# Small fp32 products on quarters of TensorE's array, and weights split before a layer's last products

## The chip, the core and the metric

The kernel is one program on one NeuronCore of a Trainium2 chip. The metric is device time in microseconds; before the change the median of three runs is 2081.71 (2081.35 to 2082.46). The engines are TensorE (PE in the profile, with its weight loads shown apart as PEld), VectorE (DVE), ScalarE (ACT), GpSimd (POOL) and SyncE (SP), which issues nearly all transfers.

## The reference, cut to what matters

Two blocks of two layers each work on a sequence of 512 tokens of width 1024; layer 0 also carries 256 tokens of context. Block one conditions both layers on a vector (`mod`). Block two adds a state space mixer, a gated linear recurrence and two feed-forward parts.

```python
# layer 0: window attention and a gated convolution, for the latent and the context tokens
mod = silu(c) @ w_ada[l] + b_ada[l]            # shift, scale, gate
q, k, v, g_a, xb, b_g, c_g, g_b = split((x * (1 + scale) + shift) @ w_in)
p = softmax([sink, q @ kc.T, q @ k_window.T]); o_a = p @ [vc, v_window]
x = layer_norm(ALPHA * x + gate * (concat(o_a * silu(g_a), o_b * silu(g_b)) @ w_out))
# layer 1: gated recurrence over chunks, S_t = diag(f_t) S_(t-1) + k_t v_t^T, both directions
# layer 2 (even): dilated attention, and a state space model over 32 groups
bu = einsum('gpc,bsgc->bsgp', b_bar, u); h = scan(a_bar, bu); y = einsum('gcp,bsgp->bsgc', c_mat, h).real
x = x + rms_norm(concat(att, ssm) @ w_out)
x = x + rms_norm((silu(xn @ w_gate) * (xn @ w_up)) @ w_down)
# layer 3 (odd): convolution, gates, scan  h_t = a_t h_(t-1) + b_t ; then a second feed-forward part
```

## The kernel before

Activations stand transposed, features on the 128 partitions and tokens along the free dimension, in tiles of 128 features. A large product is exact to about fp32 by a split: a tile `t` is held as `hi`, rounded to fp32r, and `lo = t - hi`, and `product` (three `matmul` calls for each of 8 tiles) adds hi x hi, hi x lo and lo x hi in one PSUM bank. The stationary operand is a 128x128 piece of a weight block, the moving one 512 or 256 columns of an activation tile. `weights` loads a block (512 KB) into a raw buffer `wp_r` (three of them), ScalarE copies it to `wp_h`, and VectorE or GpSimd subtracts to make `wp_l` (four buffers each).

Small products are left in fp32: the attention's probabilities times values (`po`, in `attend` of layer 0 and of the even layer), the conditioning's selection sums (`self.sel`, in `ada`), the state space kernels (`Xm` times `Cm`, in `matrices`), and the state space chunk states (`G` times `U`, in `s5_quarter`). Each is one `matmul` with a 128x128 stationary operand and 64, 2, 16 and 64 moving columns. The products of `ada` (L431) and the scores of layer 1's scans (L963) already use quarters: `tile_position=(0, 32 * k)` places a stationary operand of 32 columns in one of four column groups of the array, and its output on 32 partitions.

A layer ends in `out_products`. The first weight blocks run over all 512 columns; the last three (`keep`) run over columns 0 to 255 and then 256 to 511, so that `done` can normalise the first half while the second is multiplied. `done` needs the sum over all features of the squares (accumulated by VectorE in `po_a` or `n_a`), which TensorE forms with a matrix of ones (bank `z`). Its loop over eight tiles writes the new residual `res_x` and calls `pre`, which makes the next layer's `act_h` and `act_l`. The next layer begins in `firsts` with three blocks over the first half and then over the second, tile by tile, as the tiles become ready. The row statistic (`rms`: ones times `res_acc`, bank `z` or `g`) comes after them, since a row's factor can be applied behind a product.

The order of instructions on each engine is made by a scheduler from the program's order, priorities and its own estimates; every engine then runs its list in order, and waits on semaphores. SBUF tiles are allotted in pools, one behind the other, in steps of 32 bytes; pools of `side="right"` from the upper end.

Of the kernel before, what the change touches and what calls it, by code (L numbers as in the profile page):

```python
# [189 lines left out]
class Prog:  # L190
    def __init__(self, es, tc, I, off):
        self.tc, self.nc, self.I, self.off, self.es = tc, tc.nc, I, off, es
        nc = self.nc
        self.const = es.enter_context(tc.tile_pool(name="const", bufs=1))
        self.wp = Alloc(es, tc, "wp", {"r": (3, 1024), "h": (4, 1024), "l": (4, 1024)})
        self.dram = es.enter_context(tc.tile_pool(name="dram", bufs=1, space=bass.MemoryType.DRAM))
        self.banks = es.enter_context(
            tc.tile_pool(name="banks", bufs=1, reuse_waits="tile", space=bass.MemoryType.PSUM)
        )
        self.clock = count()  # L200
        self.used = {f"b{i}": next(self.clock) for i in range(8)}
# [103 lines left out]
    def firsts(self, ps, blocks, xs, tags=("mm",) * 3):  # L305


        ws = [self.weights(b, eng=self.nc.gpsimd) for b in blocks]
# [7 lines left out]
        return list(zip(out, ws))  # L316

# [27 lines left out]
    def out_products(self, ps, block, xs, parts, use, done, keep=3, n=1024, late=(), begun=None, spare=(None, 0)):  # L345
# [21 lines left out]
        ws = [self.weights(block(8 - keep + j), n, pool=pool if j < own else None) for j in range(keep)]  # L367
        last = iter(())
# [28 lines left out]
    def conditioning(self, es):  # L397
# [13 lines left out]
        self.sel = cond.tile([128, 2], F32, name="sel")  # L411
# [9 lines left out]
    def ada(self, l, i, p, pool=None):  # L421
# [21 lines left out]
        def finish(t=t):  # L443
# [3 lines left out]
            for a in range(2):  # L447
                self.matmul(o[:, a], t[:, a * 128:(a + 1) * 128], self.sel)
# [5 lines left out]
    def layer0(self, stop=False):  # L454

        nc, tc = self.nc, self.tc
        with ExitStack() as es:
# [78 lines left out]
            self.out_products(ps, lambda m: self.I["wo_ab"][m], xs2, PARTS, use, done, spare=(Alloc(es, tc, "w0", {"h": (1, 1024), "l": (1, 1024)}), 1))  # L536

    def layer0_mix(self, es, e0, late, xs, Y, first, s5):
# [65 lines left out]
        def attend(qT, j, n, ctx, y, sg):  # L604
# [130 lines left out]
        for j in range(4):  # L735
            ys[j] = Y("y") if j else late("y")
            cv = conv(j)
            for i in range(6):
# [80 lines left out]
    def layer1(self):  # L819
        nc, tc = self.nc, self.tc  # L820
        with ExitStack() as es:
# [24 lines left out]
            self.out_products(ps, lambda m: self.I["wo_c"][m], xs2, PARTS[:2], use, done, spare=(Alloc(es, tc, "w5", {"h": (1, 1024), "l": (1, 1024)}), 1))  # L846
# [252 lines left out]
    def prenorm(self, es, ps, name, l):  # L1099
# [8 lines left out]
        def pre(k, s, x=None, scale=g, bias=None):  # L1108
            hi, lo = self.xs[k]
# [123 lines left out]
    def s5_prepare(self, prep):  # L1233
# [111 lines left out]
        def matrices(half):  # L1345
# [3 lines left out]
            for e in range(8):  # L1349
# [27 lines left out]
                for g in range(4):  # L1377
                    self.matmul(p[:, g * 16:(g + 1) * 16], Xm[:, g * 128:(g + 1) * 128], Cm[:, g * 16:(g + 1) * 16])
# [18 lines left out]
    def s5_quarter(self, q, S, ps, ut, y):  # L1397
# [67 lines left out]
    def even(self):  # L1465
        tc = self.tc
        with ExitStack() as es:
# [6 lines left out]
            self.out_products(ps, lambda m: self.I["wo_ev"][m], xs2, PARTS[:2], use, done, late=(4, 5), begun=begun, spare=(Alloc(es, tc, "w6", {"h": (2, 1024), "l": (2, 1024)}), 2))  # L1474
            stats()

    def even_mix(self, es, e1, Y):
# [47 lines left out]
        def attend(kz, vn, qT, y, n):  # L1525
# [27 lines left out]
            for h, T in enumerate(Ts):  # L1553
                b = slice(64 * h, 64 * h + 64)
                for i in range(n + 1):
                    s = slice(i * 128, (i + 1) * 128)
                    self.matmul(po[:, b], T[:, s], vn[:, i * 128 + 64 * h:i * 128 + 64 * h + 64], i == 0, i == n)
# [130 lines left out]
    def odd(self):  # L1688
        tc = self.tc
        with ExitStack() as es:  # L1690
# [6 lines left out]
            self.out_products(ps, lambda m: self.I["wo_od"][m], xs2, PARTS[:2], use, done, late=(2, 4), spare=(Alloc(es, tc, "w7", {"h": (3, 1024), "l": (3, 1024)}), 3))  # L1697
            stats()

    def odd_mix(self, es, B):  # L1700
        nc, tc, xs, r = self.nc, self.tc, self.xs, self.rr
        A = Alloc(es, tc, "o7", {
            "sp2": (1, 8), "hb": (1, 16), "h": (4, L), "l": (4, L), "xb": (2, L + 3), "xc": (2, 1024),
# [5 lines left out]
        sp2, hb = A("sp2"), A("hb")  # L1709
# [79 lines left out]
        first = dict(enumerate(self.firsts(ps, self.od[:3], xs)))  # L1789
        self.rms(ps("g"))  # L1790
# [30 lines left out]
    def ffn(self, l, last=None):  # L1821

        nc, tc, xs, r = self.nc, self.tc, self.xs, self.rr
        with ExitStack() as es:
# [16 lines left out]
            for a, b in ((0, 6), (6, 14), (14, 22)):  # L1841
# [30 lines left out]
                else:  # L1872
# [5 lines left out]
                    self.out_products(ps, block, hs, PARTS[:2], use, done, n=n, keep=4 if last else 3, spare=(H, 2))  # L1878
# [65 lines left out]
```

## Time and profile before

| | |
|---|---|
| runs | 2081.35, 2082.46, 2081.71 us; median 2081.71 |
| profiled execution | 2084.1 us; its span 2082.1, 33162 instructions |
| busy: PE, PEld | 2008.2 us (96%), 1699.2 us (82%) |
| busy: DVE, ACT, POOL | 1307.2 us (63%), 955.9 us (46%), 386.9 us (19%) |
| granted TensorE clock, mean | 0.986 |
| DMA | 246.75 MB, 119 GB/s on average |

A TensorE instruction's duration is modelled and holds its latency, so busy times of neighbouring instructions overlap; the pace is read from start to start. An fp32 product is two instructions in the trace and one in the listed order. The chain that ended last names TensorE for 33% of the span, of which 32% is the line of `matmul` (L319).

### The profile page before, as it was taken

How to read it: one execution, taken by the hardware profiler on the slowest of the kernel's cores; microseconds unless marked ns; L12 is line 12 of the kernel's file. 1: busy time of each engine (PE TensorE's matmuls, PEld its weight loads, DVE VectorE, ACT ScalarE, POOL GpSimd, SP SyncE). 2: the span in 40 equal slices, each digit the busy share in tenths (PEclk: the TensorE clock that was granted, in tenths of full speed). 3: DMA queues.
4: the chain of work that ended last, by engine and by line, in shares of the span. 5: the costliest groups of instructions: out<-in, count | busy, mean ns of one | idle time of the engine just before them, and what ended most of it. 6: DMA issues, size and time to landing. Idle time of an engine off the chain costs nothing. (4 is left out here: it accounts for less than half of the span.)

```text
span 2082.1 us, 33162 instructions
## 1 busy us (share of the span) xinstructions
PE 2008.2 (96%) x13160; PEld 1699.2 (82%) x13160; DVE 1307.2 (63%) x2318; ACT 955.9 (46%) x1730; POOL 386.9 (19%) x383
## 2 busy tenths in 40 slices
PE   6999999999999999989999999999989999999997
PEld 4888888888888888788878878888888888888886
DVE  6775556787656665786655855544568775354455
ACT  2564333446555555554655644322346654322231
POOL 1111111335223221142102310101020131010011
PEclk9999999999999999999989999999999999999998
DMA  8344432322111111325423589333435323323331
GB/s 305 117 158 147 148 125 92 110 74 87 52 52 54 60 52 52 112 73 162 121 67 106 181 320 324 126 96 95 138 113 182 117 86 96 106 92 101 101 102 41
DMA packets 91818, 246.75 MB, mean 119 GB/s; under 512 B 20624, under 2 KB 29712, under 8 KB 91664
## 3 DMA queue, kind: packets, MB, share of 16 engines
q1 hardware_dynamic: 91664, 244.65, 35.7%
q8 instruction: 103, 1.69, 0.3%
q14 instruction: 51, 0.42, 0.1%
HBM read 209.48 MB, written 35.13 MB: 117 GB/s over the span
## 5 line engine op out<-in xcount | busy, mean ns | idle before, releaser
L245 ACT ACTIVATE wp_h<-wp_r 128x1024 fp32r<-128x1024 f32 (+2 forms) x243 | 250.9, 1037 | 416.5 <-PE mm L319 263.2
L251 DVE TENSOR_TENSOR wp_l<-wp_r,wp_h 128x1024 fp32r<-128x1024 f32 (+1 forms) x228 | 315.2, 1385 | 123.3 <-ACT wp_h L245 119.2
L319 PE MATMUL mm<-act_l,wp_h 128*128 128x512 f32 (+1 forms) x1008 | 378.9, 376 | 4.7 <-POOL act_l L251 4.7
L319 PE MATMUL mm<-act_h,wp_h 128*128 128x512 f32 (+1 forms) x1008 | 377.4, 375 | 2.5 <-ACT act_h L245 2.5
L319 PE MATMUL mm<-act_h,wp_l 128*128 128x512 f32 (+1 forms) x1008 | 377.3, 374 | 0.0
L319 PE MATMUL mm<-a_h,wp_h 128*128 128x512 f32 (+1 forms) x920 | 334.8, 365 | 5.1 <-ACT wp_h L245 3.1
L319 PE MATMUL mm<-a_h,wp_l 128*128 128x512 f32 (+1 forms) x920 | 330.1, 359 | 1.2 <-POOL wp_l L251 1.2
L319 PE MATMUL mm<-a_l,wp_h 128*128 128x512 f32 (+1 forms) x920 | 329.1, 358 | 0.6 <-DVE a_l L251 0.6
L319 PEld LDWEIGHTS mm<-act_l,wp_h 128*128 128x128 f32 x1008 | 192.3, 191 | 38.7 <-POOL act_l L251 5.8
L319 PEld LDWEIGHTS mm<-act_h,wp_h 128*128 128x128 f32 x1008 | 191.8, 191 | 35.7 <-ACT act_h L245 2.9
L319 PEld LDWEIGHTS mm<-act_h,wp_l 128*128 128x128 f32 x1008 | 192.1, 191 | 32.8 <-issue 1.0
L319 PEld LDWEIGHTS mm<-a_h,wp_h 128*128 128x128 f32 x920 | 174.1, 189 | 31.6 <-issue 3.6
L319 PEld LDWEIGHTS mm<-a_l,wp_h 128*128 128x128 f32 x920 | 174.3, 189 | 26.2 <-issue 2.3
L319 PEld LDWEIGHTS mm<-a_h,wp_l 128*128 128x128 f32 x920 | 174.0, 189 | 25.2 <-POOL wp_l L251 1.4
L251 POOL TENSOR_TENSOR g_g<-g_g,g_u 128x512 f32<-128x512 f32 x44 | 63.1, 1435 | 550.4 <-DVE g_u L251 493.7
L319 PE MATMUL mm<-h_h,wp_h 128*128 128x512 f32 (+1 forms) x344 | 129.0, 375 | 2.1 <-ACT h_h L245 2.1
L319 PE MATMUL mm<-h_l,wp_h 128*128 128x512 f32 (+1 forms) x344 | 129.2, 376 | 0.6 <-DVE h_l L251 0.5
L319 PE MATMUL mm<-h_h,wp_l 128*128 128x512 f32 (+1 forms) x344 | 128.8, 374 | 0.0
L251 DVE TENSOR_TENSOR g_u<-mm,res_rr 128x512 f32<-128x512 f32 x44 | 30.3, 689 | 110.5 <-PE mm L319 110.5
L248 ACT ACT_TABLE_LOAD x60 | 77.0, 1283 | 1.8 <-PEq L1932 0.7
L319 PEld LDWEIGHTS mm<-h_h,wp_h 128*128 128x128 f32 x344 | 64.8, 188 | 14.6 <-ACT h_h L245 3.0
L251 POOL TENSOR_TENSOR act_l<-pn_h,act_h 128x256 fp32r<-128x256 f32 x64 | 57.5, 919 | 102.6 <-ACT act_h L245 102.2
(505 smaller groups left out, 3819.2 us busy)
## 6 DMA issues: line engine op xcount, KB each, us to landing
wp_r<-w_gu SPq DMA_DIRECT2D x88, 512.0 KB, 3.6
wp_r<-w_c SPq DMA_DIRECT2D x40, 512.0 KB, 3.3
wp_r<-wada SPq DMA_DIRECT2D x32, 512.0 KB, 3.7
wp_r<-w_d SPq DMA_DIRECT2D x32, 512.0 KB, 3.5
wp_r<-w_ab SPq DMA_DIRECT2D x26, 512.0 KB, 4.6
od_d<-z_h SPq DMA_DIRECT2D x20, 512.0 KB, 3.6
od_d<-z_l SPq DMA_DIRECT2D x20, 512.0 KB, 4.0
wp_h<-od_d SPq DMA_DIRECT2D x20, 512.0 KB, 3.7
```

Source lines behind the costliest of these rows:

```text
L245: self.nc.scalar.activation(out=out, in_=in_, func=ACT.Copy, scale=scale)
L248: self.nc.scalar.activation(out=out, in_=in_, func=func, **kw)
L251: (eng or self.nc.vector).tensor_tensor(out=out, in0=a, in1=b, op=op)
L319: self.nc.tensor.matmul(out=out, lhsT=a, rhs=b, start=start, stop=stop)
```

## The change

Five things are done. `quarters` replaces `matmul` in the five small products above: four products with 32 stationary columns each, in the four column groups, over the same moving operand. `out_products` takes `after`, weight blocks of the next layer; behind the last blocks it loads and splits as many as buffers allow (`4 - keep + own`: two where one pair of spare buffers exists, else three) and `firsts` takes these over. `pre` writes the high part directly where there is no bias, with the low part as one VectorE step, and no longer uses GpSimd. In layer 0's attention a `yield` stands ahead of the value products, and the conditioning work `more_ada` is called between the two. The odd layer forms its fourth product before its statistics. Beside these, `rope2` gets a pool of its own at the upper end, and `dummy`, `sel` and `sp2` are padded to 16 elements.

```diff
-        self.rope2 = self.const.tile([128, 4], F32, name="rope2")
+        self.edge = es.enter_context(tc.tile_pool(name="edge", bufs=1, side="right"))
+        self.rope2 = self.edge.tile([128, 4], F32, name="rope2")
-        self.dummy = self.const.tile([128, 1], F32, name="dummy")
+        self.ahead = []
+        self.dummy = self.const.tile([128, 16], F32, name="dummy")[:, 0:1]
...
-        ws = [self.weights(b, eng=self.nc.gpsimd) for b in blocks]
+        ws = self.ahead + [self.weights(b, eng=self.nc.gpsimd) for b in blocks[len(self.ahead):]]
+        self.ahead = []
...
+    def quarters(self, out, a, b, start=True, stop=True):
+        for k in range(4):
+            s = slice(32 * k, 32 * k + 32)
+            self.nc.tensor.matmul(out=out[s], lhsT=a[:, s], rhs=b, start=start, stop=stop, tile_position=(0, 32 * k))
...
         ws = [self.weights(block(8 - keep + j), n, pool=pool if j < own else None) for j in range(keep)]
+        self.ahead = [self.weights(b) for b in after[:4 - keep + own]]
...
-        self.sel = cond.tile([128, 2], F32, name="sel")
+        sel = cond.tile([128, 16], F32, name="sel")
+        self.sel = sel[:, 0:2]
...
-                self.matmul(o[:, a], t[:, a * 128:(a + 1) * 128], self.sel)
+                self.quarters(o[:, a], t[:, a * 128:(a + 1) * 128], self.sel)
...
+            yield
             po = aux[:, 256:512]
...
-                    self.matmul(po[:, b], r, vn[:, tiles[i], b], i == 0, i == nk - 1)
+                    self.quarters(po[:, b], r, vn[:, tiles[i], b], i == 0, i == nk - 1)
...
-                more_ada()
                 if j:
                     next(mats, None)
+                next(at)
+                more_ada()
...
-            h = N("h")
             if bias is None:
-                self.act(h, x, ACT.Copy, scale=scale[:, k:k + 1])
+                self.act(hi, x, ACT.Copy, scale=scale[:, k:k + 1])
+                self.stt(lo, x, scale[:, k:k + 1], hi.bitcast(F32), ALU.mult, ALU.subtract)
             else:
+                h = N("h")
                 self.act(h, x, ACT.Identity, scale=scale[:, k:k + 1], bias=bias[:, k:k + 1])
-            self.copy(hi[:, s], h)
-            self.sub(lo[:, s], h, hi[:, s].bitcast(F32), nc.gpsimd)
+                self.copy(hi, h)
+                self.sub(lo, h, hi.bitcast(F32))
...
-                    self.matmul(p[:, g * 16:(g + 1) * 16], Xm[:, g * 128:(g + 1) * 128], Cm[:, g * 16:(g + 1) * 16])
+                    self.quarters(p[:, g * 16:(g + 1) * 16], Xm[:, g * 128:(g + 1) * 128], Cm[:, g * 16:(g + 1) * 16])
...
-            self.matmul(p[:, s], G[:, g], U[:, s])
+            self.quarters(p[:, s], G[:, g], U[:, s])
...
         first = dict(enumerate(self.firsts(ps, self.od[:3], xs)))
+        first[3] = proj(3), None
         self.rms(ps("g"))
```

The calls of `out_products` get `after` with the next layer's first three blocks, in the order in which `firsts` takes them; the even layer's value product changes as layer 0's does, and `sp2` is padded like `sel`.

On TensorE, in layer 0's attention before: `mc<-sel` are the selection sums, `mc<-wp_r,sc` the conditioning products, `pt` the transposes of the probabilities, `S` the scores, `x<-m_vn,m_T` the value products, `mm` a projection.

```order
L319 MATMUL mc<-sel,adat_t 128x2 x2
L657 MATMUL pt<-idn,m_P 128x128 x3
L431 MATMUL mc<-wp_r,sc 32x256 x8
L657 MATMUL pt<-idn,m_P 128x128
L319 MATMUL S<-m_kz,m_qs 128x256 x7
L657 MATMUL pt<-idn,m_P 128x128 x4
L319 MATMUL x<-m_vn,m_T 128x64 x4
L319 MATMUL S<-m_kz,m_qs 128x256
L319 MATMUL mm<-a_h,wp_h 128x512
L319 MATMUL mm<-a_l,wp_h 128x512
L319 MATMUL x<-m_vn,m_T 128x64 x4
```

The same place now:

```order
L670 MATMUL pt<-idn,m_P 128x128 x4
L326 MATMUL mc<-sel,adat_t 32x2 x8
L329 MATMUL S<-m_kz,m_qs 128x256 x3
L444 MATMUL mc<-wp_r,sc 32x256
L670 MATMUL pt<-idn,m_P 128x128 x4
L444 MATMUL mc<-wp_r,sc 32x256 x7
L326 MATMUL x<-m_vn,m_T 32x64 x32
L329 MATMUL S<-m_kz,m_qs 128x256 x5
L329 MATMUL mm<-a_h,wp_h 128x512
```

The value products of both heads stand together behind the conditioning products, in quarters as these are, and scores follow; before they stood in two groups with a score and a projection between them.

On VectorE, at the end of the first feed-forward part before, where the second half's normalisation begins: `po_t` and `po_r` are the reciprocal root, `g_ff` the mixed rows, `res_x` the residual.

```order
L267 SCALAR_TENSOR_TENSOR res_x<-g_ff,vecs,res_x 128x256
L267 SCALAR_TENSOR_TENSOR po_t<-z,po_r 128x256
L267 SCALAR_TENSOR_TENSOR po_t<-po_t,po_r 128x256
L267 SCALAR_TENSOR_TENSOR po_r<-po_t,po_r 128x256
L251 TENSOR_TENSOR g_ff<-g_ff,po_r 128x256 x2
L267 SCALAR_TENSOR_TENSOR res_x<-g_ff,vecs,res_x 128x256 x2
L251 TENSOR_TENSOR g_ff<-g_ff,po_r 128x256 x2
L267 SCALAR_TENSOR_TENSOR res_x<-g_ff,vecs,res_x 128x256 x2
L251 TENSOR_TENSOR g_ff<-g_ff,po_r 128x256 x2
L267 SCALAR_TENSOR_TENSOR res_x<-g_ff,vecs,res_x 128x256 x2
```

The same place now:

```order
L270 SCALAR_TENSOR_TENSOR res_x<-g_ff,vecs,res_x 128x256 x2
L270 SCALAR_TENSOR_TENSOR po_t<-z,po_r 128x256
L270 SCALAR_TENSOR_TENSOR act_l<-res_x,vecs,act_h 128x256 x2
L270 SCALAR_TENSOR_TENSOR po_t<-po_t,po_r 128x256
L270 SCALAR_TENSOR_TENSOR po_r<-po_t,po_r 128x256
L254 TENSOR_TENSOR g_ff<-g_ff,po_r 128x256 x2
L270 SCALAR_TENSOR_TENSOR res_x<-g_ff,vecs,res_x 128x256 x2
L254 TENSOR_TENSOR g_ff<-g_ff,po_r 128x256
L270 SCALAR_TENSOR_TENSOR act_l<-res_x,vecs,act_h 128x256 x2
L270 SCALAR_TENSOR_TENSOR res_x<-g_ff,vecs,res_x 128x256
L254 TENSOR_TENSOR g_ff<-g_ff,po_r 128x256 x2
L270 SCALAR_TENSOR_TENSOR act_l<-res_x,vecs,act_h 128x256
```

The steps that write `act_l`, which stood on GpSimd, now stand on VectorE between the residual's.

## Rows read from the trace of the kernel before

**Rows 1.** Windows: stretch and length, busy us of PE, PEld, DVE, ACT, POOL, clock, DMA.
```profile
85.00:392.00 307.00, 306.35 (x2199) 263.02 (x2198) 192.69 (x535) 143.57 (x364) 38.91 (x50) 1.00 0.40 130
500.00:862.00 362.00, 357.03 (x3925) 301.92 (x3924) 232.73 (x421) 200.29 (x366) 84.82 (x85) 1.00 0.18 57
905.00:930.00 25.00, 19.08 (x132) 17.69 (x131) 19.14 (x37) 14.99 (x34) 17.91 (x18) 0.93 0.30 93
1066.00:1087.00 21.00, 19.89 (x87) 18.13 (x87) 10.77 (x31) 7.70 (x26) 1.39 (x2) 0.51 0.08 26
1532.00:1562.00 30.00, 23.11 (x148) 20.40 (x147) 23.67 (x42) 15.99 (x36) 10.40 (x14) 0.89 0.36 136
```

**Rows 2.** Groups by line and form: shapes, count, busy us, mean ns, idle before.
```profile
L319 PE MATMUL x<-m_vn,m_T 128*128 128x64 f32 x352 | 44.8, 268 | 0.0
...
L319 PE MATMUL o<-e_vn,e_T 128*128 128x64 f32 x160 | 25.2, 302 | 0.6 <-ACT y_y L245 0.6
...
L319 PE MATMUL mc<-sel,adat_t 128*128 128x2 f32 x64 | 8.5, 238 | 0.0
...
L963 PE MATMUL a<-m_qp,m_km 128*32 128x64 f32 x256 | 5.4, 224 | 0.1
...
L319 PEld LDWEIGHTS x<-m_vn,m_T 128*128 128x128 f32 x352 | 44.4, 191 | 2.1 <-DVE m_st L626 0.4 <-DVE m_T L669 0.3
```

**Rows 3.** Timeline, weight loads of layer 0's value products: start, us for all.
```profile
305.94 0.98 PEld L319 LDWEIGHTS x<-m_vn,m_T 128*128 128x128 f32 x8
```

**Rows 4.** Timeline, TensorE in layer 1's scores: whole array, quarters, whole array.
```profile
617.44 0.28 PE L319 MATMUL mm<-a_h,wp_l 128*128 128x256 f32 x1
617.65 1.03 PE L963 MATMUL a<-m_qm,m_km 128*32 128x32 f32 x96
618.52 0.68 PE L963 MATMUL a<-m_qp,m_km 128*32 128x64 f32 x32
...
619.47 0.40 PE L319 MATMUL mm<-a_l,wp_h 128*128 128x512 f32 x1
```

**Rows 5.** Timeline, first and 24th of 512-column steps over a and over act.
```profile
872.45 0.40 PE L319 MATMUL mm<-a_h,wp_l 128*128 128x512 f32 x1
...
877.84 0.39 PE L319 MATMUL mm<-a_l,wp_h 128*128 128x512 f32 x1
...
1934.60 0.39 PE L319 MATMUL mm<-act_h,wp_h 128*128 128x512 f32 x1
...
1939.81 0.39 PE L319 MATMUL mm<-act_h,wp_l 128*128 128x512 f32 x1
```

**Rows 6.** Timeline, first and 24th of 256-column steps over a and over act.
```profile
312.79 0.28 PE L319 MATMUL mc<-a_h,wp_h 128*128 128x256 f32 x1
...
315.47 0.28 PE L319 MATMUL mc<-a_h,wp_l 128*128 128x256 f32 x1
...
1708.20 0.28 PE L319 MATMUL mm<-act_h,wp_l 128*128 128x256 f32 x1
...
1710.95 0.28 PE L319 MATMUL mm<-act_l,wp_h 128*128 128x256 f32 x1
```

**Rows 7.** Waits of TensorE over the whole span: us, times, longest us.
```profile
PE z L319 <- DVE po_a L251: 8.6, 5, 2.6
...
PE mm L319 <- POOL act_l L251: 4.7, 5, 1.2
...
PE g L319 <- DVE res_acc L251: 3.4, 1, 3.4
...
PE o L319 <- DVE res_x L267: 2.9, 1, 2.9
```

**Rows 8.** Timeline, VectorE and GpSimd at the end of the first feed-forward part.
```profile
1540.44 0.76 DVE L251 TENSOR_TENSOR g_ff<-g_ff,po_r 128x256 f32<-128x256 f32 x2
...
1541.52 5.26 POOL L251 TENSOR_TENSOR act_l<-pn_h,act_h 128x256 fp32r<-128x256 f32 x5 [3.32 <-ACT act_h L245]
...
1544.33 1.85 DVE L251 TENSOR_TENSOR g_ff<-g_ff,po_r 128x256 f32<-128x256 f32 x2
```

More of the change, by code (lines that the diff above doesn't have):

```diff
@@ L343, in scores, with out_products @@
             self.matmul(out, q[h], k[:, cols], i == 0, i == 1)
-    def out_products(self, ps, block, xs, parts, use, done, keep=3, n=1024, late=(), begun=None, spare=(None, 0)):
+    def out_products(self, ps, block, xs, parts, use, done, keep=3, n=1024, late=(), begun=None, spare=(None, 0), after=()):
         wide = [X] + [s for s in parts if s.start >= L]
@@ L535, in layer0 @@
             use, done = self.deepnorm(N, ps, res, mod, emit)
-            self.out_products(ps, lambda m: self.I["wo_ab"][m], xs2, PARTS, use, done, spare=(Alloc(es, tc, "w0", {"h": (1, 1024), "l": (1, 1024)}), 1))
+            self.out_products(ps, lambda m: self.I["wo_ab"][m], xs2, PARTS, use, done, spare=(Alloc(es, tc, "w0", {"h": (1, 1024), "l": (1, 1024)}), 1), after=[self.I["w_c"][m] for m in range(3)])
     def layer0_mix(self, es, e0, late, xs, Y, first, s5):
@@ L845, in layer1 @@
             use, done = self.deepnorm(N, ps, self.x, self.mods[1], emit)
-            self.out_products(ps, lambda m: self.I["wo_c"][m], xs2, PARTS[:2], use, done, spare=(Alloc(es, tc, "w5", {"h": (1, 1024), "l": (1, 1024)}), 1))
+            self.out_products(ps, lambda m: self.I["wo_c"][m], xs2, PARTS[:2], use, done, spare=(Alloc(es, tc, "w5", {"h": (1, 1024), "l": (1, 1024)}), 1), after=[self.I["w_ev"][m] for m in (4, 8, 0)])
             for k in range(KT):
@@ L1108, in pre @@
         def pre(k, s, x=None, scale=g, bias=None):
-            hi, lo = self.xs[k]
-            h = N("h")
+            hi, lo = (t[:, s] for t in self.xs[k])
             x = self.x[k][:, s] if x is None else x
             if bias is None:
-                self.act(h, x, ACT.Copy, scale=scale[:, k:k + 1])
+                self.act(hi, x, ACT.Copy, scale=scale[:, k:k + 1])
+                self.stt(lo, x, scale[:, k:k + 1], hi.bitcast(F32), ALU.mult, ALU.subtract)
             else:
+                h = N("h")
                 self.act(h, x, ACT.Identity, scale=scale[:, k:k + 1], bias=bias[:, k:k + 1])
-            self.copy(hi[:, s], h)
-            self.sub(lo[:, s], h, hi[:, s].bitcast(F32), nc.gpsimd)
+                self.copy(hi, h)
+                self.sub(lo, h, hi.bitcast(F32))
         def stats():
@@ L1473, in even @@
             use, done = self.postnorm(es, ps, "norm_mix_post", 0, pre)
-            self.out_products(ps, lambda m: self.I["wo_ev"][m], xs2, PARTS[:2], use, done, late=(4, 5), begun=begun, spare=(Alloc(es, tc, "w6", {"h": (2, 1024), "l": (2, 1024)}), 2))
+            self.out_products(ps, lambda m: self.I["wo_ev"][m], xs2, PARTS[:2], use, done, late=(4, 5), begun=begun, spare=(Alloc(es, tc, "w6", {"h": (2, 1024), "l": (2, 1024)}), 2), after=[self.I["w_gu0"][m] for m in range(3)])
             stats()
@@ L1556, in attend @@
                     s = slice(i * 128, (i + 1) * 128)
-                    self.matmul(po[:, b], T[:, s], vn[:, i * 128 + 64 * h:i * 128 + 64 * h + 64], i == 0, i == n)
+                    self.quarters(po[:, b], T[:, s], vn[:, i * 128 + 64 * h:i * 128 + 64 * h + 64], i == 0, i == n)
             o = E("o")
@@ L1696, in odd @@
             use, done = self.postnorm(es, ps, "norm_mix_post", 1, pre)
-            self.out_products(ps, lambda m: self.I["wo_od"][m], xs2, PARTS[:2], use, done, late=(2, 4), spare=(Alloc(es, tc, "w7", {"h": (3, 1024), "l": (3, 1024)}), 3))
+            self.out_products(ps, lambda m: self.I["wo_od"][m], xs2, PARTS[:2], use, done, late=(2, 4), spare=(Alloc(es, tc, "w7", {"h": (3, 1024), "l": (3, 1024)}), 3), after=[self.I["w_gu1"][m] for m in range(3)])
             stats()
@@ L1702, in odd_mix @@
         A = Alloc(es, tc, "o7", {
-            "sp2": (1, 8), "hb": (1, 16), "h": (4, L), "l": (4, L), "xb": (2, L + 3), "xc": (2, 1024),
+            "sp2": (1, 16), "hb": (1, 16), "h": (4, L), "l": (4, L), "xb": (2, L + 3), "xc": (2, 1024),
             "tr": (2, 1024), "ti": (2, 1024), "a": (2, L), "mu": (2, L), "u": (2, 1024), "z": (2, 1024),
@@ L1708, in odd_mix @@
         sp = self.sp
-        sp2, hb = A("sp2"), A("hb")
+        sp2, hb = A("sp2")[:, 0:8], A("hb")
         self.ts(sp2, sp, 2.0, ALU.mult)
@@ L1877, in ffn @@
                     use, done = self.postnorm(es, ps, "norm_ffn_post", l, pre, ff, last)
-                    self.out_products(ps, block, hs, PARTS[:2], use, done, n=n, keep=4 if last else 3, spare=(H, 2))
+                    self.out_products(ps, block, hs, PARTS[:2], use, done, n=n, keep=4 if last else 3, spare=(H, 2), after=() if last else self.od[:3])
                     if stats:
```

## The prediction

> **What bounds the kernel now.** I read the busy times by stretch first [rows 1]. In layer 0's attention (85 to 392 us) TensorE is busy for 306 of 307 us, in layer 1's scans for 357 of 362; VectorE has 193 and 233, ScalarE less. So there the time is the number of TensorE's instructions times their pace, and what makes them cheaper shortens the run directly. The passage from the first feed-forward to the odd layer (1532 to 1562) is different: TensorE is busy for 23 of 30 us, at a granted clock of 0.89. The list of TensorE's waits says for what [rows 7]: 8.6 us in five waits for the running sum that the last normalisation needs (po_a), 4.7 for the low parts act_l that GpSimd makes, 3.4 for res_acc before the row statistics, 2.9 for a bank that VectorE frees late. These 19.6 us lie where layers meet.
>
> Second, the small fp32 products [rows 2]. The trace has two instructions for each product, so the 352 of x<-m_vn,m_T are 176 products of attention values in layer 0, and the 160 of o<-e_vn,e_T 80 in the even layer. Three groups of 64 instructions, 32 products each, are the conditioning sums mc<-sel in layer 0's attention, the state space kernels mc<-s_C there and the chunk states s<-s_U,s_G in the even layer (the first stands for the three). Together 352 products, 704 instructions. They have 2 to 64 moving columns, and yet cost alike: eight weight loads take 0.98 us [rows 3], one lasts 0.191 [rows 2], so the pace is (0.98 - 0.19) / 7 = 0.113 us each. They pay for loading 128 columns, not for what streams past.
>
> Third, the pace of the long products [rows 5]. Twenty-four steps of 512 columns over the tiles a (layers 0 and 1) take 877.84 - 872.45 = 5.39 us between first and last, over the tiles act 1939.81 - 1934.60 = 5.21: 234 and 227 ns, with the same weights' tiles. In the built program the tiles a, b (layers 0 and 1, the even and odd outputs) and o7 begin 32 bytes past a multiple of 64; act and h begin on a multiple. 234 / 227 is 33 / 32, as if a row of 2048 bytes were fetched in pieces of 64 and one that begins in the middle needed one more. That reading is mine, from these two paces.
>
> **The change part by part.** *Quarters.* Each of the 352 products becomes four on 32 columns each, so 8 instructions. Layer 1's scores already work so: 96 of 32 moving columns go from 617.65 to 618.52, 9.1 ns each, and 32 of 64 columns last 0.68 us, of which one alone lasts 0.224: (0.68 - 0.22) / 31 = 14.8 ns [rows 2, 4]. Before: 704 x 0.113 = 79.6 us. After: 288 products of 64 columns x 8 x 14.8 ns = 34.1 us, 64 narrow ones x 8 x 9.1 = 4.7; gross gain 40.8 us.
>
> The same rows price the switch between whole array and quarters. From the last whole product (617.44) to the second one behind the block (619.47) are 2.03 us; the block's own are 0.87 + 0.47, two ordinary products 0.12 + 0.23 [rows 5, 6]; 0.34 us are left for going in and out. Read off the program's order, TensorE enters quarters 71 times instead of 20 in layer 0's attention and 27 times instead of never in the even layer: 78 x 0.34 = 26.5 us. Net 14.3 us. The narrow ones have no row of their own; with 9.1 to 14.8 ns they make up to 2.9 us less. With the switch at 0.24 to 0.44 the net is 4 to 22 us. The conditioning sums before the attention I count at nothing: that stretch waits for transfers of weights.
>
> On the price of a quarter the Trainium skill (TensorE: Matmul & The Clock Gate, section "Wait — 56ns, not 53.3ns?") speaks against the change: start to start never falls below about 25 ns, however small the product. By that, an estimate, 2816 quarters would take 70 us, and the net be a loss of 17. The trace does not agree where four column groups run side by side: 9.1 and 14.8 ns [rows 4].
>
> *Addresses.* The padding of dummy, sel and sp2 and the move of rope2 look idle, but they shift what is allotted behind them: in the built program a, b and o7 now begin on multiples of 64. 2088 instructions of 512 columns stream from them. At the difference of [rows 5], 0.18 us in 23 steps, that is 7.8 ns each, 16 us. The 256-column products go the other way: 23 steps over a take 315.47 - 312.79 = 2.68 us, over act 1710.95 - 1708.20 = 2.75 [rows 6], 3.0 ns more, and 2112 of them stream from the moved tiles: 6.3 us lost, if the address is the reason there too (their pace is near that of weight loads, so it may not be). I take the lower, 16.3 - 6.3 = 10, of which I count 9; ends 0 and 16.
>
> *Between layers.* Three things happen. (a) Three weight blocks (two where only one spare pair of buffers exists) are split on ScalarE and VectorE ahead of the last products, no longer on GpSimd behind them. (b) The low parts act_l move from GpSimd to VectorE, and ScalarE writes the high part in one step instead of two. (c) The odd layer does its fourth product before its statistics.
>
> For (a) and (b) VectorE gets 16 instructions per passage at the 0.38 us of an undisturbed one (two in 0.76), 6.1 us. It loses a disturbance: while GpSimd makes act_l (5.26 us for five), two of VectorE's last 1.85 [rows 8]. GpSimd is busy for 10.4 us of that passage, which slows some 11 of VectorE's by 0.55: 6 us. So VectorE ends about when it did. But TensorE has more in front of the wait: in the order z<-po_a stands behind 36, 30 and 30 first products instead of 29, 19 and 19, 29 x 0.12 = 3.5 us of the 8.6. Of the 4.7 us for act_l I take half, 2.4: the chain is one hop shorter, but VectorE makes them at 3 x 0.4 us per tile against 1.08 us that TensorE needs for nine products. Of the 2.9 us for the bank, held up by a weight split on GpSimd, 1.5, since the third block there is still GpSimd's. For (c): 24 products x 0.227 = 5.4 us now cover the 3.4 us, but then the reciprocal root and its three VectorE steps stand uncovered, because the four banks hold products that wait for it; net 2. The clock: 0.89 over 30 us means 30 x 0.11 x 2 = 6.6 us at half clock, and 0.93 over 25 us (layer 1 to the even layer, [rows 1]; the passages behind the even and the odd mixer read alike) 3.5 each, 17 us in all, and idle stretches stand before them. If half of it stays away, that is 8.5 us and gives back at most half, 4.3; some of it is waiting anyway, so 3. Sum 12.4; ends -4 (VectorE late in each passage) and 26 (all waits and most of the half clock).
>
> The added waits: SyncE now issues the ahead transfers in front of the next layer's, and each must find one of three raw buffers free; ScalarE's split waits for that transfer with squares and act_h queued behind it. The cover is the wide products just before, 24 x 0.227 = 5.4 us each, with VectorE half idle. Without that cover each block would cost its split, some 1 us. The new yield in the attention moves the value products behind the conditioning work; it lets the transposes' copies finish and costs nothing.
>
> **Sum.** The profiled execution took 2084.1 us, 2.0 more than its span and 2.4 more than the median of 2081.7. 2084.1 - 14.3 - 9 - 12.4 = 2048.4; less 2.4, 2046 as a median.
>
> **The rivals.** *VectorE becomes the bound at the passages* (15%). For: it is busy for 23.7 of 30 us there and gets all low parts. Against: GpSimd's disturbance goes. The 12.4 become -4: 2062.
> *The pace does not follow the address* (9%). For: only two kinds of tiles are compared, and 256 columns say the opposite. Against: the ratio 33 / 32. 2055.
> *Short runs of quarters do not reach that pace* (4%). For: layer 0's blocks have 16 to 64 instructions, layer 1's 128. Against: 32 already gave 14.8. Priced with the whole 0.68 / 32 = 21.3 ns each, 2816 take 60 us: 60 + 26.5 - 79.6 = 7 us lost instead of 14 gained, 2067. (By the Trainium skill's 25 ns, same page and section, it would be 2077.)
> *The half clock spreads* (6%), the one on the other side. From 1066 to 1087 the even layer's attention, almost all small products, ran at 0.51 [rows 1], which gives up about half of each us. The quarters make the array's work in layer 0's attention thinner, 307 us at 1.00 now. It decides from 72 us granted half: 72 x 0.5 = 36, the whole gain. A third of the stretch, 102 us, gives 2046 + 51 = 2097. Against: layer 1 has quarter blocks in 362 us at a clock of 1.00, and long products lie between.
> *The half clock of that even stretch goes or shrinks* (12%): its 44 small instructions alone take 10 us at half clock: 2035.
>
> **How the numbers follow.** The forecast has 54%, by itself 2032 to 2060. With the neighbours the range of 8 in 10 is 2027 to 2069: below it lies the case that all waits and the half clock go, above it the spread of the half clock. A measurement of this kernel tells 0.2%, 4.2 us, from no change. Faster by more: forecast, VectorE, address, even stretch and short runs, less their tails: 0.91. Within: 0.03. Slower: 0.06, the spread of the half clock.
>
> **What would show it.** Small products s<-s_U,s_G, x<-m_vn and o<-e_vn in quarters at 9 to 15 ns, and about 0.34 us per change of shape; runs of 24 products over a and b at 227 ns; z<-po_a waits of some 5 us in all and no act_l from GpSimd; the odd layer's g without a wait, the next product waiting instead. Wrong would be: the granted clock under 1.00 in layer 0's attention, 234 ns still over a, or VectorE over 27 of 30 us busy at the passages with longer waits of TensorE behind it.

## The result, and the profile after

The changed kernel takes 2055.34 us in the median of four runs (2051.76 to 2056.33), the kernel before 2081.53 (2079.78 to 2082.46): 0.9871 of the time, 95% interval 0.9855 to 0.9886, or 26 us less. The forecast was 2046 with a range of 2027 to 2069. Direction and range hold, the gain is about ten short of the forecast's 36.

TensorE does the same long products in both traces, so where the time went can be read from their starts: I took the same product at each border of two parts and noted by how much it comes earlier.

| part | gained, us | forecast's term |
|---|---|---|
| conditioning and first products | 1.9 | nothing |
| layer 0's attention | 4.5 | quarters, addresses |
| layer 0's output products | 0.6 | addresses |
| layer 0 to layer 1 | -3.1 | between layers |
| layer 1 | 0.7 | addresses |
| layer 1 to the even layer | 4.3 | between layers |
| even layer | 6.9 | quarters, addresses |
| even layer to feed-forward, and its beginning | 3.6 | between layers |
| feed-forward to the odd layer | 3.8 | between layers |
| odd layer | 0.5 | addresses |
| odd layer to the last feed-forward part | 3.5 | between layers |

They add up to 27.2. The passages between layers bring 12.1, forecast 12.4. All the rest brings 15.1, forecast 23.3 for quarters and addresses: that is where the difference lies.

The waits of TensorE in the changed kernel (us in total, times, longest):

```profile
PE z L329 <- DVE n_a L254: 4.6, 3, 3.5
PE mm L329 <- DVE o_xb L254: 3.7, 1, 3.7
...
PE mc L444 <- DVE mod L254: 3.4, 3, 1.7
...
PE mm L329 <- ACT act_h L251: 2.7, 1, 2.7
...
PE z L329 <- DVE po_a L254: 1.9, 1, 1.9
PE o L329 <- DVE res_x L270: 1.9, 1, 1.9
```

Against [rows 7] the wait for po_a falls from 8.6 to 1.9 us, act_l is gone, res_acc in front of g too; in its place the odd layer's next product waits 3.7 us for o_xb, as foretold. The third line has grown: conditioning products (mc) in layer 0's attention wait for mod, an addition on VectorE that reads the bank of the selection sums. Before it was

```profile
PE mc L431 <- DVE mod L251: 0.2, 1, 0.2
```

The stretches of [rows 1], where they stand now (length, busy us of PE, PEld, DVE, ACT, POOL, clock, DMA):

```profile
83.00:386.00 303.00, 296.36 (x3640) 241.78 (x3639) 197.07 (x536) 138.28 (x360) 41.90 (x50) 1.00 0.41 132
496.00:858.00 362.00, 357.04 (x3928) 302.99 (x3927) 232.91 (x421) 200.97 (x367) 84.76 (x85) 1.00 0.19 58
900.00:922.00 22.00, 19.55 (x143) 18.91 (x142) 21.47 (x52) 15.33 (x35) 6.71 (x5) 0.92 0.36 107
1050.00:1071.00 21.00, 16.94 (x292) 12.84 (x292) 17.87 (x45) 11.84 (x34) 2.67 (x3) 1.00 0.10 26
1510.00:1538.00 28.00, 25.38 (x181) 23.31 (x179) 23.57 (x59) 12.27 (x25) 0.10 (x1) 1.00 0.41 147
```

In layer 0's attention TensorE's idle time rose from 0.7 of 307 us to 6.6 of 303. Layer 1 takes its 362 us as before. The even stretch that ran at a clock of 0.51 runs at 1.00, but TensorE now idles there for 4 of 21 us.

The small products, timeline of one quarter block in layer 0's attention (start, us for all):

```profile
270.58 0.39 PE L329 MATMUL mm<-a_h,wp_h 128*128 128x512 f32 x1
270.90 0.88 PE L326 MATMUL x<-m_vn,m_T 128*32 128x64 f32 x48
271.71 0.50 PE L329 MATMUL mm<-a_l,wp_h 128*128 128x512 f32 x1
272.05 0.39 PE L329 MATMUL mm<-a_h,wp_l 128*128 128x512 f32 x1
```

From the long product before the block to the second one behind it are 1.47 us. Two products of 0.23 leave 1.01; the block's 48 instructions begin within 0.66 (0.014 each, from 0.88 less the 0.22 that one lasts), and 0.35 go for the change of shape. Both prices of the forecast stand: 14.0 ns against 14.8, and 0.34 us.

The pace of 512 columns over a in layer 1, first and 24th of a run:

```profile
868.46 0.40 PE L329 MATMUL mm<-a_h,wp_l 128*128 128x512 f32 x1
...
873.81 0.40 PE L329 MATMUL mm<-a_l,wp_h 128*128 128x512 f32 x1
```

5.35 / 23 = 232.6 ns. It was 234 [rows 5] and should have become 227, although a now begins on a multiple of 64.

### The profile page after: what moved, and what is told of

Same layout as the page of the kernel before. It is cut to its first block, busy times and chain, and to the rows that moved or that the text cites. A ratio compares the mean times of both kernels' runs of the same rounds, so it can differ in the third digit from the quotient of the medians.

```text
span 2054.5 us, 37475 instructions
## 1 busy us (share of the span) xinstructions
PE 1977.6 (96%) x15368; PEld 1654.0 (81%) x15368; DVE 1305.1 (64%) x2392; ACT 940.1 (46%) x1682; POOL 305.5 (15%) x309
## 4 chain that ended last, share of the span: by engine, by line
PE 69%; DVE 14%; ACT 6%; issue 6%; POOL 2%; DMA 2%; SPq 0%; POOLq 0%; DVEq 0%; ACTq 0%
PE mm L329 57%; PE a L329 2%; PE mc L329 2%; DMA wp_r<-w_ab 1%; PE S L329 1%; ACT wp_h L248 1%; PE a L978 1%; PE s L329 1%; DVE s_b L254 1%; PE mc L444 1%; PE x L326 1%; ACT L251 1%; PE z L329 1%; POOL m_ks L254 1%; PE pt L670 1%
## 5 line engine op out<-in xcount | busy, mean ns | idle before, releaser
L254 DVE TENSOR_TENSOR wp_l<-wp_r,wp_h 128x1024 fp32r<-128x1024 f32 (+1 forms) x238 | 325.8, 1369 | 141.4 <-ACT wp_h L248 137.4
L329 PE MATMUL mm<-act_l,wp_h 128*128 128x512 f32 (+1 forms) x1008 | 374.5, 373 | 0.0
L329 PEld LDWEIGHTS mm<-h_l,wp_h 128*128 128x128 f32 x344 | 64.8, 188 | 13.5 <-DVE h_l L254 2.1
```

Source lines behind the costliest of these rows:

```text
L254: (eng or self.nc.vector).tensor_tensor(out=out, in0=a, in1=b, op=op)
L329: self.nc.tensor.matmul(out=out, lhsT=a, rhs=b, start=start, stop=stop)
```

## The experiments

**The three parts one by one.** Three kernels, each the kernel before with one part of the change. The first has only the padding:

```diff
-        self.rope2 = self.const.tile([128, 4], F32, name="rope2")
+        self.edge = es.enter_context(tc.tile_pool(name="edge", bufs=1, side="right"))
+        self.rope2 = self.edge.tile([128, 4], F32, name="rope2")
-        self.dummy = self.const.tile([128, 1], F32, name="dummy")
+        self.dummy = self.const.tile([128, 16], F32, name="dummy")[:, 0:1]
...
```

> The kernel before with nothing but the padding (dummy, sel, sp2 to 16 columns, rope2 on the right side). Theory P (the prediction: a start on a multiple of 64 takes 33/32 away): 512 columns over a, b and o7 at 227 ns instead of 234, about 9 us less, 2072. Theory W (read from the changed kernel's trace: the pace depends on where the moving tile lies against the weights' tiles, modulo 512 bytes; 227 at distance 0, about 230 at 64, 232 at 128, 233 to 234 at 32, 160 and 192): a0 at 230, a1 and b at 232, o7 at 233, 256 columns about 0.5 to 1 ns slower, in all 3 to 4 us less, 2078. Third: no effect, 2081.5.

Measured: 0.9979 (0.9966 to 0.9992) of the time before, 1.7 to 7.1 us less. The mean step of 512 columns goes from 232.8 to 229.7 ns over a0, 234.1 to 232.4 over a1, 233.9 to 232.9 over b2, 233.9 to 233.2 over o7. None reaches 227. Theory P falls.

The second has only the quarters and the yield:

```diff
-                    self.matmul(po[:, b], r, vn[:, tiles[i], b], i == 0, i == nk - 1)
+                    self.quarters(po[:, b], r, vn[:, tiles[i], b], i == 0, i == nk - 1)
...
```

> The kernel before with the quarters at their five places and the yield that goes with them, nothing else. Theory of the prediction: 14 us less, 2067, half clock of the even stretch as before. Theory from the changed trace: the gross gain and the 0.34 us per change of shape are as forecast, but in layer 0's attention TensorE now waits for conditioning sums and transposes (about 5 us more than before), and in the even layer the half clock goes (10 us) while later waits give part of it back; together 10 to 12 us less, about 2070. If all the gain were the half clock of the even stretch, layer 0's attention would end no earlier and the time be about 2075.

Measured: 0.9963 (0.9950 to 0.9975), 5 to 10 us less, not 14. Its half clock in the even attention is gone.

The third has only the work between layers:

```diff
-        ws = [self.weights(b, eng=self.nc.gpsimd) for b in blocks]
+        ws = self.ahead + [self.weights(b, eng=self.nc.gpsimd) for b in blocks[len(self.ahead):]]
...
+        first[3] = proj(3), None
```

> The kernel before with the work between layers alone: weights split ahead, act_l on VectorE, the odd layer's fourth product before its statistics. Theory (prediction and changed trace agree): 12 us less, 2069; the passage from layer 0 to layer 1 loses 3 us (a wait for n_a of 3.5 us and a half clock that follows it), the five others win 15. Rival: the gain of the passages comes from where the quarters left the work of VectorE, then 6 us or less, 2076. If the three single parts (e1, e2, e3) are independent their gains add up to 26 us.

Measured: 0.9941 (0.9925 to 0.9957), 9 to 16 us less, middle 12. The waits are those of the whole change (z for po_a 1.9 us, mm for o_xb 3.8). Of layer 0 to layer 1 the expectation was wrong: no loss there, n_a makes TensorE wait 2.9 us as before. The loss of 3 us in the changed kernel's profile comes with one wait of 3.5 us and a half clock behind it (463 to 470 us) that this run doesn't have. From the first z<-n_a to layer 1's first product the nine profiles without a half clock there take 46.0 to 47.1 us, the kernel before among them, the five with one 48.0 to 49.7; so this loss isn't fixed to the change. The three parts give 4.4 + 7.7 + 12.3 = 24 us, against 27 together (1 - 0.9871 of 2081.5): within the intervals, nothing speaks against adding them.

**What sets the pace of the long products.** In the changed kernel's built program the weights' tiles, act and h begin at 320 modulo 512 bytes, a0 at 384, a1 and b at 448, o7 at 0. So a tile's distance from the weights could count. First all five moved to 320:

```diff
+            self.pad(self.es1, "a", 32)
             self.a1 = Alloc(self.es1, tc, "a1", ...)
...
-            "sp2": (1, 16), ...
+            "sp2": (1, 96), ...
```

Here pad takes so many columns on the right side in front of the tile; sel goes into the tile of rope2, which moves a0.

> The changed kernel with a0, a1, b2, b3 and o7 moved so that they begin at the same place modulo 512 bytes as the weights' tiles (320), as act and h already do. Theory W (distance to the weights): all products of 512 columns over a, b, o at 227 ns, 10 us less, and the 256-column ones at 120 instead of 116 to 119, 4 us more: 6 us less in all, 2049. Theory P (only the multiple of 64 counts) or a reason in the tiles' shape: paces stay at 230 to 233 and the time at 2055.

Measured: 0.9861 (0.9841 to 0.9880), which the time can't tell from the changed kernel. The trace can: the usual (median) step over a0, a1, b and o7 is 227 ns, and the mean of 256 columns (with the tiles wp) lies at 119.4 to 120 instead of 116 to 119. Layer 0's attention ends 2 us later, mostly by that (its 256-column steps over a0 take 1.8 us more), layer 1 gains 3.0 us instead of 0.7, and at the end the same products come 3.9 us earlier than in the changed kernel. Theory W told paces and signs; the gain of 6 was 4 in the profile and isn't resolved in the time.

Two more kernels, of one run each, settle the rule. One moves a1, b2, b3 and o7 to other distances:

```diff
+            self.pad(self.es1, "a", 96)
...
+                self.pad(es, "b", 64)
...
```

> The changed kernel with other distances to the weights' tiles, modulo 512: a1 256, b2 384, b3 448, o7 320 bytes (a0 64 as before). Theory W: only the distance sets the pace of 512 columns, so that each of the four shows a pace of its own between 227 and 234 ns, and none of the four 227; all lie on multiples of 64. Rival (multiple of 64 and something in the tiles themselves): a1 and b stay at 232, o7 at 233.

a1, 256 bytes from the weights' place, runs at 227 ns (median), b2 at 384 at 232.9, b3 at 448 at 233.3, o7 at 320 at 229.6. So the expectation that none of them reaches 227 was wrong in one point that tells more: 256 is as good as 0, 320 as 64, 384 as 128. What counts is the distance modulo 256 bytes.

The other moves the weights instead, with act and h, by 64 bytes (sel goes into the tile of rope2 again, so that a0 stays):

```diff
-        self.dummy = self.const.tile([128, 16], F32, name="dummy")[:, 0:1]
+        self.dummy = self.const.tile([128, 32], F32, name="dummy")[:, 0:1]
...
```

> The changed kernel with the weights' tiles, act and h 64 bytes further (384 modulo 512); a0 stays at 384, a1 and b at 448, o7 goes to 64. Theory W, distance counts: a0 at distance 0 goes to 227 ns, a1 and b at distance 64 to about 230, act and h stay at 227, o7 (192) at 233. Rival, the absolute place counts: a0 stays at 230 and act and h go to 230, a1 and b stay at 232.

Timeline of this kernel, 13 steps over a0 and 22 over act, first and last:

```profile
303.54 0.39 PE L330 MATMUL mm<-a_h,wp_l 128*128 128x512 f32 x1
...
306.26 0.39 PE L330 MATMUL mm<-a_h,wp_l 128*128 128x512 f32 x1
...
1984.64 0.39 PE L330 MATMUL mm<-act_h,wp_l 128*128 128x512 f32 x1
...
1989.40 0.39 PE L330 MATMUL mm<-act_h,wp_l 128*128 128x512 f32 x1
```

2.72 / 12 and 4.76 / 21 are both 226.7 ns. The place of a0 itself is the same as in the changed kernel, whose 13 steps there take 2.75:

```profile
303.12 0.39 PE L329 MATMUL mm<-a_h,wp_l 128*128 128x512 f32 x1
...
305.87 0.39 PE L329 MATMUL mm<-a_h,wp_l 128*128 128x512 f32 x1
```

That is 229.2 ns. The weights moved and a0's pace changed; act moved along with them and kept its own. a1 at 64 now has 229.7, o7 stays at 192 with 233.3. The rival of the absolute place falls.

**Where layer 0's quarters went.** The sum of the forecast for that attention: 472 instructions x 0.113 - 1376 x 0.014 - 512 x 0.009 - 49 x 0.34 = 12.8 us (counts from the trace's records), and the addresses some 1.7 (540 steps of 512 columns x 3.2 ns). Gained were 4.5. In three parts, before (columns as above):

```profile
78.80:155.40 76.60, 76.27 (x550) 64.76 (x551) 60.67 (x158) 50.11 (x106) 9.63 (x18) 1.00 0.41 140
155.40:275.40 120.00, 119.54 (x880) 101.24 (x880) 66.18 (x197) 45.82 (x128) 14.02 (x20) 1.00 0.44 140
275.40:389.60 114.20, 114.20 (x788) 99.85 (x787) 71.56 (x200) 49.56 (x139) 14.71 (x13) 1.00 0.32 102
```

and the same work in the changed kernel:

```profile
76.90:154.40 77.50, 72.87 (x834) 60.57 (x835) 64.04 (x163) 46.98 (x103) 14.04 (x18) 1.00 0.44 146
154.40:269.80 115.40, 114.71 (x1449) 93.96 (x1447) 66.22 (x192) 44.07 (x126) 11.86 (x18) 1.00 0.45 140
269.80:383.20 113.40, 112.03 (x1355) 90.51 (x1355) 72.24 (x199) 49.35 (x139) 14.61 (x13) 1.00 0.32 102
```

TensorE's busy time falls by 10.4 us (310.0 to 299.6), its idle time rises by 5.9, of which 4.3 in the first part. The 10.4 are some 4 short of 12.8 + 1.7, because the whole products had been cheaper than priced. Start to start, waits left out, the 472 instructions take 48.7 us in the trace before, 103 ns each, and not 53.3: in nearly every block of value products the first step is about 57 ns and the last 84, and only those between are 112. One block of eight, and what follows it:

```profile
306.06 1.00 PE L319 MATMUL x<-m_vn,m_T 128*128 128x64 f32 x8
306.87 0.37 PE L319 MATMUL S<-m_kz,m_qs 128*128 128x256 f32 x1
```

0.81 / 8 = 101 ns.

In the first part VectorE is busy for 64 of 77 us, since it also makes the rotary products and the state space preparation, and the stretch takes 0.9 us longer than before. The wait for mod comes with the quarters: the kernel with quarters alone has 2.5 us of it in that part, the three kernels without quarters 0.2. Behind the 3.4 us for mod, the longest waits of TensorE in the changed kernel's attention:

```profile
PE pt L680 <- DVE m_T L673: 1.5, 3, 0.9
PE x L326 <- DVE m_T L673: 0.9, 2, 0.5
```

Is it the order that the yield makes, mod's place in VectorE's queue, or VectorE as a whole? Three kernels ask. The yield taken out:

```diff
             nc.vector.reciprocal(out=sk[:, 2:4], in_=sk[:, 0:2])
-            yield
...
-                next(at)
-                more_ada()
```

(more_ada stands in front of next(mats, None) again.)

> The changed kernel without the new yield: in layer 0's attention the conditioning sums stand in front of the transposes again, the value products right behind them. Theory Y: the yield put the addition mod behind softmax and state space work in VectorE's queue, and TensorE's next conditioning product waits for it (mc for mod 3.4 us, in the kernel before 0.2; with the waits for m_T 5.8 us against 0.7); without it 4 to 5 us come back, 2051. Rival: the quarters of the values then wait for the copies m_T in each of 24 blocks, 0.2 to 0.5 us each, 5 to 12 us, less the 3 us of mod: 2057 to 2064.

Measured: 0.9875 (0.9855 to 0.9894), nothing against the changed kernel's 0.9871. The wait for mod is longer, not shorter:

```profile
PE mc L444 <- DVE mod L254: 4.7, 2, 2.8
PE pt L680 <- DVE m_T L673: 1.3, 3, 0.6
```

and the last transpose of the attention comes 3.6 us later. Theory Y falls, its rival too (no new waits of x). The yield costs nothing. Whether it saves something isn't shown: a half clock from 147 to 150 us lies in this run and not in the changed kernel's, and the times are the same.

The addition taken from VectorE:

```diff
-            self.add(self.mods[l][:, m, :], o, self.bada[:, l, m, :])
+            if pool:
+                self.add(self.mods[l][:, m, :], o, self.bada[:, l, m, :])
+            else:
+                self.copy(t[:, 0:4], p[:, 0:4])
+                self.add(self.mods[l][:, m, :], t[:, 0:4]..., self.bada[:, l, m, :], self.nc.gpsimd)
```

> The changed kernel with the addition mod of layer 0's attention taken from VectorE: ScalarE copies the four columns from the bank, GpSimd adds. Theory Q (a matter of the queue: the bank comes free late because mod stands behind other work on VectorE): TensorE's 3.4 us of waits for mod go, about 3 us less, 2052, if nothing stands behind them. Theory V (VectorE is the bound there): the waits move to m_T, m_qs or m_q, the first quarter of the attention ends as late, 2055.

Measured: 0.9874 (0.9852 to 0.9896), the same time. The waits in its attention:

```profile
PE x L326 <- DVE m_T L677: 4.8, 4, 2.7
PE pt L684 <- DVE m_T L677: 2.7, 3, 1.2
PE x L702 <- ACT m_o L251: 1.2, 2, 0.9
```

No wait for mod is left, and those for m_T, VectorE's other work, grew from 2.4 to 7.5 us. That speaks for theory V; that the last transpose comes even 2.6 us later is not explained by it alone (a half clock from 145 to 152 us lies in this run). VectorE isn't busy throughout (64 of 77 us), so it is the bound in spots: in the changed kernel's trace it has no gap over 0.11 us in the 4 us before each of the three waits for mod and before the longest one for m_T.

And the quarters taken out of the first six blocks:

```diff
-                    self.quarters(po[:, b], r, ...)
+                    (self.matmul if j == 0 else self.quarters)(po[:, b], r, ...)
```

> The changed kernel with the attention values of layer 0's first head pair (j = 0, six blocks) on the whole array again; the quarters stay everywhere else. By the sum the quarters save there 80 x 0.113 - 320 x 0.014 - about 6 x 0.34 = 2.5 us of TensorE's work. Theory V (VectorE, busy for 64 of the 77 us, sets the pace of that first part, so what TensorE saves there is spent in waits): the transposes m_P a quarter through the attention come as before (154.4 us, within 0.5), and TensorE waits less for mod and m_T. Rival (the waits come from the order alone, the quarters' gain is on the path): they come 2 to 3 us later.

In one run 2055.56 us, the changed kernel's time; the first part takes 78.8 us instead of 77.5, TensorE is busy for 76.7 of them:

```profile
76.60:155.40 78.80, 76.71 (x594) 64.32 (x595) 63.81 (x163) 49.40 (x105) 12.75 (x20) 1.00 0.47 150
```

3.8 us more work of TensorE make the part 1.3 longer, between what the two theories expect. In this run two thirds of what these quarters save is spent waiting. But the kernel before, whose value products are whole there too, takes 76.6 us for the part, 2.2 less than this one. So shorter value products are not all of it: in both kernels with the change five more instructions of VectorE (163 against 158, more of the state space preparation) stand in the part, 3 us more of its work, and the selection sums are quartered. No run separates these.

**The even layer.** Its two groups on the whole array again:

```diff
-            self.quarters(p[:, s], G[:, g], U[:, s])
+            self.matmul(p[:, s], G[:, g], U[:, s])
...
```

> The changed kernel with the even layer's two groups (chunk states s, attention values o) on the whole array again, quarters everywhere else. By the forecast's sum the even layer's quarters gave 224 x 0.113 - 896 x 0.014 - 27 x 0.34 = 3.6 us, and a half clock of 20 us that goes was to be worth 10 more. Theory C: with the whole products the half clock of the even attention (1066 to 1087 us before) is back, and yet the layer loses only 6 to 7 us, 3 to 4 of work and 2.6 of clock, since softmax and normalisation on VectorE and ScalarE bound that stretch too: 2062. Rival 1: the clock stays up, 3 to 4 us lost, 2059. Rival 2: the half clock is back and costs its full 10 us, 2068.

Measured: 0.9901 (0.9880 to 0.9921), 2060.96 us. The granted clock is at half again, from 1058 to 1075 us. The end of the layer's attention and scans in the kernel before:

```profile
1066.00:1113.00 47.00, 45.14 (x232) 39.01 (x233) 22.70 (x56) 27.40 (x65) 6.25 (x5) 0.78 0.13 42
```

in this one:

```profile
1055.00:1105.00 50.00, 47.33 (x262) 40.90 (x261) 25.32 (x59) 30.65 (x70) 7.64 (x6) 0.83 0.13 43
```

and in the changed kernel:

```profile
1050.00:1099.00 49.00, 43.13 (x503) 32.07 (x502) 29.66 (x71) 36.39 (x79) 6.54 (x6) 1.00 0.12 36
```

The stretches don't begin at the same product. Between two fixed ones (the 46th s<-s_H and the last s<-act) lie 59.6 us before, 58.2 here, 57.0 in the changed kernel. So 17 to 20 us at half clock cost at most 1.3 to 2.6 us, since these differences hold whole against quartered products too. At full clock TensorE is idle for 6 of 49 us there, waiting for e_st, b_h and s_h. Theory C holds, with 5.6 us lost of its 6 to 7; both rivals fall.

**A faster version.** The distances chosen by what is streamed. Modulo 256, 64 is best where as many 256-column products stream as 512-column ones (229.6 + 116 ns, against 226.7 + 120), 0 where there are only long ones. First with the yield out and a1, b2, b3, o7 at 0, in the belief in theory Y:

```diff
-            yield
...
+            self.pad(self.es1, "a", 32)
...
```

> The changed kernel without the yield and with a1, b2, b3 and o7 at the weights' place modulo 512 bytes; a0 stays 64 bytes off, where 256 columns ran at 116 ns and 512 at 230. If theory Y and the distance to the weights both hold and add up: 4 to 5 us from the yield and about 6 from layer 1 on (as the run with all five moved showed behind layer 0), 2045. If only one of them holds, 2050; if neither, 2055.

Measured: 0.9870 (0.9851 to 0.9889), no gain: without the yield layer 0's attention ends 2 us later, and of the 2.9 us that layer 1 gains (0.7 in the changed kernel) a half clock in the even layer takes a part back. Then with the yield, a1, b2 and b3 at 64 as a0, o7 at 0:

```diff
+            self.pad(self.es1, "a", 16)
...
+                self.pad(es, "b", 16)
...
+            self.pad(es, "c", 16)
...
-            "sp2": (1, 16), ...
+            "sp2": (1, 32), ...
```

> The changed kernel with a1, b2 and b3 64 bytes from the weights' place modulo 256 (as a0) and o7 at distance 0. If the distance sets the pace: 512 columns over a in layer 1 and over b at 229.6 ns instead of 232.4, 256 columns at 116.5 instead of 119, o7 at 227 instead of 233; about 3 + 1.5 us in layer 1, 0.7 in the even layer, 1.5 in the odd one: 6 to 7 us less than the changed kernel, 2049. If the gain of these paces is lost in waits: 2053 to 2055.

Measured: 2047.84 us (2046.93 to 2051.0), 0.9841 (0.9822 to 0.9860) of the time before, some 6 us below the changed kernel (their intervals overlap by a hair; in its profile the same products come 9.3 us earlier at the end, 3.7 of them from the passage to layer 1, where no half clock fell; that passage differs from profile to profile, as said above). The run of 24 over a1:

```profile
861.62 0.39 PE L335 MATMUL mm<-a_h,wp_h 128*128 128x512 f32 x1
...
866.89 0.39 PE L335 MATMUL mm<-a_h,wp_l 128*128 128x512 f32 x1
```

5.27 / 23 = 229.1 ns, 232.6 in the changed kernel; 256 columns over a in layer 1 go from 118.9 to 116.4.

## Why the prediction was right, and where it was off

*Between layers, 12.4 forecast, 12.3 (9 to 16) measured.* The sum was right, its terms less so. z for po_a gave 6.7, not 3.5; act_l all of its 4.7, but act_h still costs 3.3 against 2.5; the odd layer gave nothing, since o_xb's 3.7 us took the place of the 3.4 before g, where a gain of 2 was counted.

*Quarters, 14.3 forecast, 7.7 (5 to 10) measured.* The price of a quarter, 14.0 ns, and of a switch, 0.35 us, were right where the blocks were read. Two steps failed. The 113 ns of a whole product were read between eight weight loads in a row and taken for all; in layer 0 it was 103 on average, 4.6 us less to save. And "busy for 306 of 307 us ... so there the time is the number of TensorE's instructions times their pace": true as far as VectorE keeps up, and in the first 77 us of that attention it doesn't, by a few us. The mean of 193 of 307 us hid a first part with 61 of 77. Whether VectorE is late there for the amount of its work or for its order stays open. Waits took 5.9 us back: 12.8 + 1.7 - 4.6 - 5.9 = 4.0, of the 4.5 us gained. So of the 12.8 us for layer 0 some 3 came through. The even layer made up for part of it: 5.6 us between the medians, which the intervals don't quite resolve, and 5.5 between the same products of the two profiles, instead of 3.6.

*Addresses, 9 forecast, 4.4 (2 to 7) measured.* The padding does shorten the long products, but the reason was wrong. "As if a row of 2048 bytes were fetched in pieces of 64" explained two paces; the runs show a rule on the distance to the weights. The move took a0 from 32 to 64, a1 and b from 160 to 128, o7 from 160 to 192: 3 ns, 1.7 and under 1 instead of 7. The 256-column products lost less than the 3 ns that were feared. Sign and place of the term were right, its size half.

*The rivals.* That the pace doesn't follow the address would have been 2055, and that is the time, but for another reason: it does follow it, only not to 227, and the quarters fell short too. VectorE became the bound, though not at the passages, where the rival stood (23.6 of 28 us and short waits), but in spots of layer 0. The half clock of the even stretch did go, which was priced at 10 us more; it gave at most 2.6, and TensorE then waits for others there. A half clock that spreads did not come: 1.00 in layer 0's attention.

By the Trainium skill (TensorE: Matmul & The Clock Gate, section "Wait — 56ns, not 53.3ns?") the quarters would have cost 25 ns each, an estimate by which the change loses; the trace has 14.0 ns over 48 of them in a row, and the kernel with quarters alone is faster.

## What to carry to other kernels

A stretch where TensorE is busy for 99% can be held by another engine as soon as TensorE has a few per cent less to do: cut it into parts before pricing a saving, and ask in each which queue is next. The price of small products that stand between other work is read over all their blocks, ends included, not inside one. A half clock that goes away need not give back half of its stretch: here TensorE then waited for others. And a pace that differs between two tiles is best tried at four or five places before a rule is read from it.

## What the runs showed of the hardware that was not expected

The step of a 512-column product in fp32r depends on where the streamed tile begins against the loaded weights' tile, modulo 256 bytes. Means over all such steps of the runs, start to start, waits left out:

| distance, bytes | 512 columns, ns | 256 columns, ns |
|---|---|---|
| 0 (act, h) | 226.7 | 120 |
| 32 (a0 before) | 232.8 | 117 |
| 64 (a0 after; a1, b in the last version; o7 at 320) | 229.6 | 116 |
| 128 (a1, b after; b2 at 384) | 232.5 | 119 |
| 160 (a1, b, o7 before) | 234.0 | 118 |
| 192 (o7 after; b3 at 448) | 233.3 | 115 |

The 512-column steps agree to some 2 ns between tiles at the same distance. The 256-column ones are those of the main group at each distance; others lie up to 3 ns away (118 and 115 at 192), so for them this is no rule.

Open is why, and one exception: in the even layer's products where the weights stream and act is loaded (S and pt from wp), both tiles begin at the same place, and yet the step is 235 ns. The loaded piece there is every fourth column of act, beginning 0 to 12 bytes in, so it isn't the same access; no run separates the two.

And 17 to 20 us of small products at half clock in the even attention come in every profile without that layer's quarters (four of four) and in none with them (ten of ten, shorter pieces aside).
